# Sampled sequences: both heads' products of the incoming state in one step; shorter gaps between recurrence steps, with a bank booked apart from the gap

## The chip, the cores and the metric

The kernel runs on one core of a Trainium2 chip. A core has a matrix engine (TensorE; PE in the profile), three engines for elementwise work (VectorE or DVE, ScalarE or ACT, GpSimd or POOL) and DMA queues (SyncE or SP issues most of them). The metric is the device time of one execution in microseconds (us). The kernel before took 1620.5 us, the median of three runs that lie between 1619.76 and 1621.67.

## The reference, cut to what matters

One layer of a decoder trunk is computed for a prompt of 1024 tokens and for eight sampled sequences of 8 tokens, which share all weights. The part that the change touches is the RWKV-7 recurrence: eight heads of 64 channels, each with a 64x64 state.

```python
P = h @ lp["w_in"]
pr, pp, pg = jnp.split(P, [RWKV_COLS, RWKV_COLS + POOL_WIDTH], axis=-1)
o_r, s_shift, s_wkv, v_first = rwkv7_branch(pr, shift0[l], wkv0[l], v_first, lp)
o_p, s_pool = pool_branch(pp, pool0[l], pos0, lp)

def step(S, inp):                       # inside rwkv7_branch, once per token
    r_t, w_t, k_t, v_t, kk_t, a_t = inp
    sa = jnp.einsum("bhvk,bhk->bhv", S, -kk_t)
    S = (S * w_t[:, :, None, :]
         + sa[..., None] * (kk_t * a_t)[:, :, None, :]
         + v_t[..., None] * k_t[:, :, None, :])
    y = jnp.einsum("bhvk,bhk->bhv", S, r_t)
    return S, y
```

The prompt starts from a zero state. Each sampled sequence starts from a given state (`state_wkv`), so its 8 tokens need the products of r and of kk with that incoming state.

## The kernel before

**Two phases.** The tokens (1024 + 64 = 1088 columns) lie along the free dimension, features on the 128 partitions. Phase 1 multiplies by `w_in`, 34 blocks of 128 output columns, and runs the recurrence and the pooling branch among these products. Phase 2 (branch products, output projection, feed-forward, final norm) starts with products that read the recurrence's result. Every dense product is made of float32r matmuls in three terms (`mm3`: high x high, high x low, low x high), on three chunks of 362 to 364 columns. They write the PSUM tiles `mm`.

**The recurrence.** Two heads at a time share the 128 partitions (`HB` = partitions 0-63 and 64-127), so there are four head pairs, f = 0 to 3. The prompt goes in chunks of 64 tokens. Per head pair the steps are:
- `front` and `burst`: decays, keys and so on, elementwise and some products.
- `scores`: `unit(0)`, `bonus`, `unit(2)`, `unit(1)`. Units 0 and 1 are eight prompt chunks each, unit 2 is the sampled tokens. A unit makes its score products in groups of four chunks (two groups for a prompt unit, one for unit 2), each group into two PSUM banks, one a head; then it scales the keys in place (`bh`), transposes values and keys, and makes one more product.
- `inverse` (VectorE) and `level` (small 32x32 products): a triangular inverse.
- `affine`: `first(0)`, `second(0)`, `first(1)`, `second(1)`, each with two banks; they turn a chunk into one affine map of the state.
- `chain`: sixteen dependent steps through these maps. It keeps the two `wc` banks for itself meanwhile (`pace.held`).
- `sample`: the sampled tokens, from the incoming state `s0` (64 rows a head, 512 columns: 8 sequences x 64). `post`: group norm and gating.

**The order on TensorE is written out by the program.** TensorE's instructions keep the order in which the Python code issues them; the other engines are ordered by the framework. `Pace` is a planner that decides that order as the program is built. It keeps a clock `t` of estimated TensorE time, moved on by each matmul. `Pace.run` has one background generator (the dense products; each `yield` is one group of three matmuls) and four foreground generators, in this order: `chains`, `pools`, `heads`, `or_rows`. A foreground generator yields either a number of nanoseconds, and is due that much later, or a condition. Whenever a foreground generator is due it makes its next step; otherwise one more dense group is issued. So the number after a step is the distance, filled with dense products, to the next one.

**Two generators in one.** `both(a, fill)` merges two foreground generators into one, with `a` first. In `heads`, `lead` (burst and scores of f) goes with `sample(f-1)`, and `main` (inverse, level, affine of f) with `fill` (post of f-1, then front of f+1). For f = 0 `lead` runs alone, without `both`.

**Banks.** The recurrence, pooling and sampling steps share four PSUM banks, two called `w` and two called `wc`. `ps("w")` takes the one that the planner thinks is free first (`take`). After a step, `give` books each taken bank as free again at t + r, where r is the number that the step yields (at least 1500, at most 3600); for a step inside `both` it is `pace.gap`, which `both` sets to that same number. `free` says whether any bank is free by that estimate, and a step of `heads` inside `both` waits for it. Nothing of this is a hardware wait; the true waits are semaphores, and a step that is issued before its bank or data is ready makes TensorE wait.

The numbers that the change touches stand in `unit` (`yield 3500` after each score group), `affine` (`yield 3600` after `second`) and `sample`. Matmuls are all recorded at L204 (`mm`), transposes at L211 (`tr`); the copies and sums that empty the banks have lines of their own: L855 to L863 for the score groups, L1093 and L1100 for `sample`, L684 for the pooling steps, L1163 and L1184 for `post`.

Of the kernel before, what the change touches and what calls it, by code (L numbers as in the profile page):

```python
# [83 lines left out]
class Pace:  # L84
# [3 lines left out]
    def __init__(self):  # L88
        self.t = 0.0
        self.work = []  # L90
        self.dense = False
        self.taken, self.banks, self.gap, self.held = None, {"w": [0.0, 0.0], "wc": [0.0, 0.0]}, 1500, False

    def take(self):

# [6 lines left out]

    def free(self):
        return min(self.banks[x][0] for x in (["w"] if self.held else ["w", "wc"])) <= self.t

    def give(self, r):
        for tag in self.taken:
# [24 lines left out]
    def run(self, back, fore=(), until=lambda: False):  # L132
        self.back = back
        live = {i: 0.0 for i in range(len(fore))}
        busy = True
        while (live or busy) and not until():
            for i in sorted(live):
                r = live[i]
                if self.taken is not None and i and not self.free() and (i == 2 and not isinstance(r, Off) and not hasattr(r, "own") or i == 1 and not callable(r) and self.t < r + 1200):
                    continue  # L140
                if r() if callable(r) else r <= self.t:
                    if self.taken is not None:
                        self.taken, self.gap = [], 1500
                    try:
                        r = next(fore[i])
                        if self.taken:
                            self.give(min(max(self.gap if callable(r) else r, 1500), 3600))
                        live[i] = r if callable(r) else type(r)(self.t + r)
                    except StopIteration:
                        del live[i]  # L150
                    break
            else:
                r = "idle"
                if busy:
                    try:
                        r = next(back)
                    except StopIteration:
                        busy = False
                self.dense = r != "idle"
                if r == "idle" and live:  # L160
                    self.t += 100
# [9 lines left out]
class K:  # L171
# [647 lines left out]
    def unit(self, f, d, u):  # L819
# [22 lines left out]
        for a in range(0, C, 4):  # L842
# [3 lines left out]
            pss = [self.ps("w") for _ in HB]  # L846
# [4 lines left out]
            for h, (hs, ps) in enumerate(zip(HB, pss)):  # L851
                os = HB[1 - h]
# [4 lines left out]
                for b in range(2):  # L857
# [5 lines left out]
                            nc.scalar.activation(ao[rq, cu, :], pa[rq, :, 32:64], AF.Copy)  # L863
                    else:
                        nc.vector.tensor_tensor(ad[rq, 16, :], src[:, 0, :], strict[rq, 32 * b:32 * b + 32], op=ALU.mult)
            yield 3500
        bh = bk[:, cs, :, :].rearrange("p c s j -> p c (s j)")
        if prompt:
            nc.vector.tensor_tensor(bh, bh, end[:, cs].unsqueeze(2).to_broadcast([P, C, 128]), op=ALU.mult)
# [4 lines left out]
        ps, pa = self.ps("w"), self.ps("w") if prompt else None  # L874
        for i in range(C):
            for h, hs in enumerate(HB):
                c, os = c0 + i, HB[1 - h]
                self.mm(ps[hs, i * 64:(i + 1) * 64], v[hs, c * 64:(c + 1) * 64], ident[hs, hs], start=True, stop=True)
        if prompt:
            for i in range(C):  # L880
                for h, hs in enumerate(HB):
                    os = HB[1 - h]
# [6 lines left out]
        for a in range(0, C, 4):  # L889
            m = min(4, C - a)  # L890
            ps = self.ps("w")
# [4 lines left out]
        if prompt:  # L896
            yield 800
            ps = self.ps("w")
            for i in range(C):
                for h, hs in enumerate(HB):  # L900
                    os = HB[1 - h]
# [90 lines left out]
    def affine(self, f, d):  # L992
# [35 lines left out]
        for u in range(2):  # L1028
            first(u)
            yield 2500  # L1030
            second(u)
            self.done.add(("s", f, u))
            yield 3600

    def chain(self, f, d):

# [39 lines left out]
    def sample(self, f, d):  # L1076
# [14 lines left out]
            os = HB[1 - h]  # L1091
            self.mm(px[os, 0:64], ak[hs, 0, :], uv[hs, 0, h, :], start=True, stop=True, tile_position=(hs.start, os.start))
        nc.scalar.activation(x2, px[:, 0:64], AF.Copy)  # L1093
        for h, hs in enumerate(HB):
            os = HB[1 - h]
            if h:
                yield 2500
            ps, um = self.ps("w"), iv()
            self.mm(ps, ra[hs, 0, :, :].rearrange("p s j -> p (s j)"), s0[hs, :], start=True, stop=True)
            nc.vector.tensor_tensor(qv(um), qv(ps), qm.unsqueeze(2).to_broadcast([P, 8, 64]), op=ALU.mult)  # L1100
            nc.vector.tensor_reduce(xr[:, h, :], um.rearrange("p (q v) -> p v q", v=64), axis=AX.X, op=ALU.add)
            nc.vector.tensor_tensor(x[os], xr[os, h, :], x2[os], op=ALU.add)
        yield 9500 if f < 3 else 8000
        px = self.ps("w")
        for os in HB:
            self.mm(px[os, 0:64], z[os, 16, :], x[os, :], start=True, stop=True)
# [145 lines left out]
    def both(self, a, fill):  # L1252

        pace = self.pace
        live = [[a, pace.t], [fill, pace.t]]
        now = lambda: [x for x in live if (x[1]() if callable(x[1]) else x[1] <= pace.t) and (isinstance(x[1], Off) or pace.free())]
        some = lambda: bool(now())
        some.own = True
        while live:
            ready = now()  # L1260
            if not ready:
                yield some
                continue
            x = ready[0]
            try:
                r = next(x[0])
                x[1] = r if callable(r) else type(r)(pace.t + r)
                if pace.taken:
                    pace.gap = 1500 if callable(r) else r
                    yield some  # L1270
            except StopIteration:
                live.remove(x)
# [51 lines left out]
    def iv(self):  # L1324
        return self.p1.tile([P, 32, 32], F32, tag="iv", bufs=2, name=self.nm("iv"))
# [730 lines left out]
NC = 17  # L2056
FH = [(0, 512), (512, 576)]
FP = [(0, 512), (512, 288), (800, 288)]
LS = (2000, 2000, 2000, 1500)
FW = 5500  # L2060
WB = (2, 2)
# [77 lines left out]
```

## Time and profile before

| | |
|---|---|
| median of three runs | 1620.5 us |
| the profiled execution | 1620.03 us, its span 1618.2 us |
| mean granted TensorE clock | 0.996 of full speed |
| ScalarE, GpSimd busy | 736.1 us, 356.5 us |
| 64x512 products of `sample` (w<-hv,ra) | 16 instructions, 641 ns each in the middle |
| 64x64 products of `chain` (wc<-S,ra and wc<-ra,S) | 240 + 240 instructions, 218 ns each |

A profile row of the timeline gives start, duration, engine, line, operation, output tile <- input tiles, shape, and in brackets the idle time before it and what ended it. Tile names are the program's: `hx` and `whi`/`wlo` are dense products, `ra`, `ab`, `ak`, `uv`, `at`, `bk`, `z` belong to the recurrence, `px` and `plw` to pooling, `wt` is a row buffer and `hv` a scratch tile (in `sample` it is `s0` and the masked products). A matmul of float32 is two instructions, and one of less than 128x128 uses a part of the array. Rows of a table by windows give the window, the length, busy time (and count) of the engines asked for, the granted clock, the DMA share and GB/s; with all engines the order is PE, PEld, DVE, ACT, POOL.

### The profile page before, as it was taken

What the parts mean: (1) busy time and instruction counts of PE and PEld (TensorE: products, weight loads), DVE (VectorE), ACT (ScalarE), POOL (GpSimd) and SP (SyncE); (2) the same over time, 40 slices, a digit from 0 to 9 for tenths busy, and PEclk for the clock granted to TensorE, in tenths of its full rate; (3) what the DMA queues carried; (4) which work ended last, traced back from release to release, by engine and by line L of the source; (5) the groups of instructions that cost most, each with busy time, mean ns of one, the idle gap of its engine ahead of it and who ended that gap; (6) DMA issues with size and microseconds to landing.
All of it is one profiled execution on the core that took longest, in us unless ns stands there. A gap on an engine that the chain in (4) does not pass through costs nothing.

```text
span 1618.2 us, 35474 instructions
## 1 busy us (share of the span) xinstructions
PE 1583.4 (98%) x14331; PEld 1481.7 (92%) x14331; DVE 1022.9 (63%) x1747; ACT 736.1 (45%) x1491; POOL 356.5 (22%) x464
## 2 busy tenths in 40 slices
PE   5999999999999999999999999999999999999997
PEld 3999888998898889979989999999999999999997
DVE  5685674846565636244635597777555777787866
ACT  5543343344335433432325475554455765553323
POOL 3301200120001000101513322333233243521231
PEclk9999999999999999999999999999999999999998
DMA  9334423423423242746875466667666865674313
GB/s 336 110 119 145 140 65 107 132 83 115 126 101 115 76 138 89 294 144 216 332 261 175 144 199 215 206 223 256 234 209 234 312 201 186 197 265 154 100 40 111
DMA packets 123333, 279.43 MB, mean 173 GB/s; under 512 B 16769, under 2 KB 31105, under 8 KB 123169
## 3 DMA queue, kind: packets, MB, share of 16 engines
q1 hardware_dynamic: 107808, 228.52, 41.7%
q0 software_dynamic: 9312, 32.41, 6.0%
q10 hardware_dynamic: 6048, 16.23, 2.8%
q8 instruction: 113, 1.85, 0.5%
q14 instruction: 52, 0.42, 0.1%
HBM read 198.15 MB, written 78.95 MB: 171 GB/s over the span
## 4 chain that ended last, share of the span: by engine, by line
PE 61%; DVE 2%; issue 2%; ACT 2%; DMA 1%; POOL 1%; DVEq 0%; SPq 0%; ACTq 0%; POOLq 0%
PE pr L204 30%; PE mm L204 22%; PE w L204 4%; PE wc L204 4%; DVE hx L1815 0%; DMA wr<-in_w_ff 0%; POOL wlo L228 0%; PE wc L211 0%; DVE hx L1984 0%; DMA wraw<-in_w_ff 0%; PE w L211 0%; POOL wr L1788 0%; DMA d_th<-px 0%; ACT hx L1738 0%; ACT mr L1738 0%
## 5 line engine op out<-in xcount | busy, mean ns | idle before, releaser
L204 PE MATMUL mm<-hx,whi 128*128 128x362 f32 (+1 forms) x1920 | 504.8, 344 | 0.8 <-ACT px L573 0.8
L204 PEld LDWEIGHTS mm<-hx,whi 128*128 128x128 f32 x1920 | 330.1, 189 | 34.0 <-issue 16.1
L204 PE MATMUL pr<-mr,whi 128*128 128x272 f32 x1792 | 336.4, 287 | 0.5 <-DVE hx L1815 0.2
L204 PE MATMUL mm<-hx,wlo 128*128 128x362 f32 (+1 forms) x960 | 314.1, 327 | 0.0
L204 PEld LDWEIGHTS pr<-mr,whi 128*128 128x128 f32 x1792 | 280.8, 188 | 2.7 <-issue 2.7
L204 PE MATMUL pr<-mr,wlo 128*128 128x272 f32 x896 | 257.9, 288 | 0.0
L227 ACT ACTIVATE whi<-wraw 128x512 fp32r<-128x512 f32 x186 | 116.8, 629 | 222.1 <-PE mm L204 86.3
L228 DVE TENSOR_TENSOR wlo<-wraw,whi 128x512 fp32r<-128x512 f32 x145 | 107.5, 742 | 132.2 <-ACT whi L227 130.3
L204 PEld LDWEIGHTS mm<-hx,wlo 128*128 128x128 f32 x960 | 181.3, 189 | 0.0
L204 PE MATMUL pr<-hx,whi 128*128 128x272 f32 x896 | 168.8, 287 | 1.4 <-DVE rs L2010 0.8
L204 PEld LDWEIGHTS pr<-mr,wlo 128*128 128x128 f32 x896 | 168.6, 188 | 0.2 <-DVE wlo L228 0.2
L204 PE MATMUL mm<-mr,whi 128*128 128x272 f32 (+4 forms) x736 | 152.3, 301 | 0.0
L204 PEld LDWEIGHTS pr<-hx,whi 128*128 128x128 f32 x896 | 140.3, 188 | 2.7 <-ACT whi L227 1.0
L227 ACT ACTIVATE whi<-wr 128x512 fp32r<-128x512 f32 x138 | 86.3, 627 | 113.8 <-PE pr L204 76.3
L204 PE MATMUL pr<-hx,wlo 128*128 128x272 f32 x448 | 128.9, 288 | 0.0
L204 PEld LDWEIGHTS mm<-mr,whi 128*128 128x128 f32 x736 | 119.2, 188 | 3.0 <-issue 2.5
L204 PE MATMUL mm<-mr,wlo 128*128 128x272 f32 (+4 forms) x368 | 110.1, 299 | 0.0
L228 POOL TENSOR_TENSOR wlo<-wraw,whi 128x512 fp32r<-128x512 f32 x41 | 54.8, 1337 | 217.8 <-ACT whi L227 217.6
L228 DVE TENSOR_TENSOR wlo<-wr,whi 128x512 fp32r<-128x512 f32 x103 | 76.7, 747 | 18.3 <-ACT whi L227 18.2
L204 PE MATMUL pr<-t,whi 128*128 128x272 f32 x448 | 84.6, 287 | 0.0
L204 PEld LDWEIGHTS pr<-hx,wlo 128*128 128x128 f32 x448 | 84.3, 188 | 0.0
L204 PEld LDWEIGHTS pr<-t,whi 128*128 128x128 f32 x448 | 70.2, 188 | 0.8 <-issue 0.8
(466 smaller groups left out, 2711.0 us busy)
## 6 DMA issues: line engine op xcount, KB each, us to landing
wr<-in_w_ff SPq DMA_DIRECT2D x137, 256.0 KB, 3.5
hid<-d_ch POOLq DMA_DIRECT2D x72, 272.0 KB, 3.9
wraw<-in_w_ff SPq DMA_DIRECT2D x71, 256.0 KB, 3.2
wraw<-in_w_in SPq DMA_DIRECT2D x68, 256.0 KB, 3.1
d_ch<-hx SPq DMA_DIRECT2D x52, 272.0 KB, 3.8
hid<-in_w_ada_mlp SPq DMA_DIRECT2D x24, 512.0 KB, 6.5
d_th<-px SPq DMA_DIRECT2D x22, 544.0 KB, 3.1
wt<-d_x SPq DMA_DIRECT2D x20, 544.0 KB, 4.2
```

Of the source, the lines that this page charges most:

```text
L204: return self.nc.tensor.matmul(out, lhsT, rhs, **kw)
L227: nc.scalar.activation(hi, raw, AF.Copy)
L228: (nc.gpsimd if pool else nc.vector).tensor_tensor(lo, raw, hi.bitcast(F32), op=ALU.subtract)
```

## The change

`sample` issued the product of the two 64x64 operands and head 0's product of the incoming state in one step, and head 1's 2500 ns later. Now the 64x64 product goes alone, and 800 ns later both heads' products of the state go next to each other, into two banks; VectorE's work on each follows. The next step comes 11000 (9500 for f = 3) after that instead of 9500 (8000) after head 1's.

In `unit` the gap after a score group goes from 3500 to 2000, and in `affine` the gap after `second` from 3600 to 500. A new field `pace.est` lets a step inside `both` book its banks for another time than its gap: 3500, 3600 and 3600 at these three places. A step that is due then still waits in the planner for a bank that is free by estimate.

There are also a method `soon`, which may put off a step of the later generators where another one is due within `PAIR` ns, and the due time `some.due` that it reads; `PAIR` is 0.

```diff
@@ Pace.__init__
+        self.est = None
@@ Pace
+    def soon(self, live, i):
+
+        if not self.dense or i == 1:
+            return False
+        ts = [getattr(r, "due", lambda: None)() if callable(r) else None if isinstance(r, Off) else r for j, r in live.items() if j != i and j < 3]
+        return any(t is not None and self.t < t <= self.t + PAIR for t in ts)
@@ Pace.run
                 if r() if callable(r) else r <= self.t:
+                    if self.taken is not None and not isinstance(r, Off) and self.soon(live, i):
+                        continue
@@ unit
-            yield 3500
+            self.pace.est = 3500
+            yield 2000
@@ affine
             second(u)
             self.done.add(("s", f, u))
-            yield 3600
+            self.pace.est = 3600
+            yield 500
@@ sample
         nc.scalar.activation(x2, px[:, 0:64], AF.Copy)
-        for h, hs in enumerate(HB):
-            os = HB[1 - h]
-            if h:
-                yield 2500
-            ps, um = self.ps("w"), iv()
+        yield 800
+        pss = [self.ps("w") for _ in HB]
+        for hs, ps in zip(HB, pss):
             self.mm(ps, ra[hs, 0, :, :].rearrange("p s j -> p (s j)"), s0[hs, :], start=True, stop=True)
+        for h, ps in enumerate(pss):
+            os, um = HB[1 - h], iv()
             nc.vector.tensor_tensor(qv(um), qv(ps), qm.unsqueeze(2).to_broadcast([P, 8, 64]), op=ALU.mult)
             nc.vector.tensor_reduce(xr[:, h, :], um.rearrange("p (q v) -> p v q", v=64), axis=AX.X, op=ALU.add)
             nc.vector.tensor_tensor(x[os], xr[os, h, :], x2[os], op=ALU.add)
-        yield 9500 if f < 3 else 8000
+        self.pace.est = 3600
+        yield 11000 if f < 3 else 9500
@@ both
+        some.due = lambda: min([x[1] for x in live if not callable(x[1]) and not isinstance(x[1], Off)], default=None)
...
                 if pace.taken:
-                    pace.gap = 1500 if callable(r) else r
+                    pace.gap = pace.est or (1500 if callable(r) else r)
+                    pace.est = None
                     yield some
@@ constants
+PAIR = 0
```

## The prediction

> **What bounds it.** I read the engine table first, then TensorE's waits between 60 and 760 us (the stage in which the recurrence runs among the projections), then that stage's timeline.
>
> ```profile
> span 1618.2 us, 35474 instructions
> PE 1583.4 (98%) x14331; PEld 1481.7 (92%) x14331; DVE 1022.9 (63%) x1747; ACT 736.1 (45%) x1491; POOL 356.5 (22%) x464
> ...
> PE wc L211 <- DVE px L684: 1.4, 1, 1.4
> PE wc L204 <- DVE wt L1184: 1.1, 1, 1.1
> PE w L204 <- ACT hv L979: 0.9, 1, 0.9
> ...
> PE wc L204 <- ACT wt L333: 0.5, 1, 0.5
> PE wc L204 <- ACT wt L725: 0.4, 1, 0.4
> PE w L204 <- ACT wt L1163: 0.4, 1, 0.4
> PE wc L204 <- DVE px L684: 0.3, 1, 0.3
> ```
>
> TensorE works 98% of the span. From the first score group to the recurrence's end it waits seven times, 5.0 us in all. So the end is set by the sum of what TensorE does, not by the length of the recurrence: a step that goes sooner lets a projection product go later, and the sum stays. The end of the stage says the same:
>
> ```profile
> 737.82 0.27 PE L211 MATMUL w<-kct,sw 128*128 128x128 f32 x1
> ...
> 741.74 1.38 DVE L1202 TENSOR_TENSOR hx<-wt,hx 128x576 fp32r<-128x576 f32 x1
> ...
> 753.42 0.49 PE L204 MATMUL w<-hx,whi 128*128 128x362 f32 x2
> ```
>
> The recurrence's last TensorE work is at 737.8, its result is in SBUF at 743.1, and the first product that reads it starts at 753.4. There are 10 us of slack already, all filled with projection products. More slack buys nothing.
>
> **Part 1: both heads' products of the incoming state in one step (sample).** Each product multiplies 64 rows of the state, 512 columns wide. Before, they go 3.8 us apart. In the same shape the front step issues its w2 and a2 products side by side, on rows 0-63 and 64-127, into two banks:
>
> ```profile
> 548.62 0.33 PE L204 MATMUL w<-uv,ak 64*64 64x64 f32 x4
> 548.88 1.12 PE L204 MATMUL w<-hv,ra 64*128 64x512 f32 x2
> 549.93 0.59 PE L204 MATMUL mm<-hx,whi 128*128 128x362 f32 x2
> ...
> 552.70 1.12 PE L204 MATMUL w<-hv,ra 64*128 64x512 f32 x2
> 553.75 0.33 PE L204 MATMUL wc<-S,ra 64*64 64x64 f32 x4
> ...
> 534.56 0.69 PE L204 MATMUL w<-wt,sw 64*128 64x512 f32 x1
> 534.57 0.69 PE L204 MATMUL wc<-wt,sw 64*128 64x512 f32 x1
> 535.10 0.59 PE L204 MATMUL w<-wt,sw 64*128 64x512 f32 x1
> 535.10 0.59 PE L204 MATMUL wc<-wt,sw 64*128 64x512 f32 x1
> 535.62 0.60 PE L204 MATMUL mm<-hx,whi 128*128 128x362 f32 x2
> ...
> L204 PE MATMUL w<-hv,ra x16: 589/641/693, 231.0 to 700.1; 64*128 64x512 f32 x16
> ```
>
> One state product alone takes 548.88 to 549.93, 1.05 us, and the other 552.70 to 553.75, again 1.05. The front's pair takes 534.56 to 535.62, 1.06 us for both: the two halves of the array worked at once. The new step issues its two products adjacent, on the same two row halves, into two banks, so 2.10 becomes 1.06. The x16 are two instructions for each of eight products, so four head pairs gain: 4 x 1.04 = 4.2 us off TensorE's path. The number of visits to small tiles stays at two (the old first visit held the 64x64 product and head 0; now that product goes alone). The ends are 0 (the products run one after another) and 4.2; I take 4.2 because the front's rows have the same shape, rows and form.
>
> By the Trainium skill ("TensorE: Matmul & The Clock Gate", section "Step-by-step: what each phase is for") TensorE pulls weight loads ahead but keeps matmuls in program order. By that rule the second instruction of head 0 would hold back the first of head 1; the rows at 534.56 and 534.57, of two different products, do not look like it. What it would make of the sum is the in-order rival below.
>
> The second of the two banks may be the one that the 64x64 product has just filled, since the chain of states keeps the two "wc" banks at that time:
>
> ```profile
> 549.71 0.24 ACT L1093 ACTIVATE x<-w 128x64 f32<-128x64 f32 x1
> ```
>
> It is emptied at 549.95, 1.3 us after that product began. The new step starts at least two 0.5 us groups of projection products after it (800 ns of the planner), at about 1.4 us: no wait to 0.2 us, and I take nothing. The old wait for ACT L1163 (0.4) belongs to the same place in the last head and may go; I leave it among the re-drawn ones. VectorE's work on the products is the same six steps, and the next consumer is 11 us of the planner's time off.
>
> **Part 2: score groups 2000 apart instead of 3500, affine 500 instead of 3600.** Nothing is added to any engine; five gaps per head pair shrink by 1.5 us and two by 3.1 us. Their steps wait for a bank estimate of 3500 or 3600 only where no bank is free. Is the data there when they go?
>
> ```profile
> 295.80 0.37 PE L204 MATMUL w<-ra,bk 64*128 64x128 f32 x1
> ...
> 300.56 0.37 PE L204 MATMUL w<-ra,bk 64*128 64x128 f32 x1
> ...
> 300.21 0.27 ACT L861 ACTIVATE iv<-wc 32x128 f32<-32x128 f32 x1
> ...
> 305.45 0.97 PE L204 MATMUL wc<-kct,wt 64*64 64x64 f32 x26
> ```
>
> Here the groups start 4.8 us apart; after it, about 3.3. The second group takes the other two banks. The transposes at 305.45 come about 3 us sooner, at 302.5, and reuse the first group's banks, empty at 300.5: 2 us of margin. In head pairs 1 to 3 the step is hidden this way; their first unit has only two banks (the chain holds the rest) and stays nearly as it is. Head pair 0 is tighter, VectorE being crowded there:
>
> ```profile
> 80.00:120.00 40.00, 39.95 (x307) 36.38 (x307) 34.80 (x55) 18.48 (x47) 3.36 (x12) 1.00 0.36 119
> ...
> 117.42 1.23 DVE L869 TENSOR_TENSOR bk<-bk,end 128x1024 f32<-128x1024 f32 x1
> ...
> 120.24 0.60 PE L211 MATMUL w<-kct,bk 128*128 128x128 f32 x4
> ...
> 179.50 1.94 DVE L935 STREAM_TRANSPOSE iv<-iv 128x512 f32<-128x512 f32 x2
> 183.37 0.82 PE L204 MATMUL w<-hv,hv 32*32 32x32 f32 x74
> ```
>
> The scaled keys are ready at 118.65 and TensorE transposes them at 120.24, 1.6 us later. Two gaps ahead of that transpose shrink by 3.0 us; if VectorE (87% busy in this slice) does not move its work up, TensorE waits 1.4 us. The inverse ends at 181.4 and its first product starts at 183.4: 2.0 us of margin, of which one gap (1.5) lies between the last scores and it, so at most a fraction of a microsecond there. Both together are 0 to 1.9 us; I take 0.7, a little under the middle, as VectorE takes ready work first in most rows. In the affine steps the first product of the second half needs nothing of the step just before it; the cover of two banks emptied since the first half is 5 us old by then. Nothing.
>
> **Part 3: what does nothing.** PAIR is 0, so soon() asks for a due time that is later than now and not later than now: it never holds a step back, and due only feeds it. The est field only books banks. In head pair 0 the leading steps do not go through both(), so their banks are booked for 2000 and not 3500; that is within the 1.4 us above. No DMA is added or moved past another by hand; the loads of the next head pair go earlier on SP with its steps, and no wait of TensorE in this stage is for a DMA.
>
> **Part 4: the waits are drawn anew.** Every recurrence step after 106 us shifts against the pool steps, so the seven waits above (5.0 us) will stand elsewhere. The worst is a pile-up at 504 to 512, where a pool step, a spread and a level step fall due together with no projection between them:
>
> ```profile
> 504.00:508.00 4.00, 3.05 (x69) 1.00 0.00 0
> 508.00:512.00 4.00, 2.62 (x29) 0.83 0.43 135
> 512.00:516.00 4.00, 4.00 (x61) 0.74 0.07 21
> 680.00:684.00 4.00, 4.00 (x116) 1.00 1.02 416
> ```
>
> It idles 0.95 + 1.38 = 2.3 us, and the granted clock then falls to 0.83 and 0.74 for 4 us each, 0.7 + 1.0 us more: 4.0 in all. With the clock, 6.7 us are drawn anew. None of them may come back, or twice as much; I take the same again, 0, since as many steps meet as before.
>
> **The sum.** -4.2 + 0.7 + 0 = -3.5 us. The profiled execution took 1620.03 us (1618.2 of span and 1.8 around it), 0.5 under the median 1620.5 and within its three runs: 1616.5 us.
>
> **Rivals.** *In-order products* (the two products of the new step overlap only in their middle instruction): three half products of 0.53, 1.58 instead of 2.10, gain 2.1; 1620.0 - 2.1 + 0.7 = 1618.6. The front's four rows speak against it, and that the matmuls' ends are modelled speaks a little for it.
> *The pile-up goes*: its 4.0 us do not come back elsewhere, 1612.5. For it: one coincidence in the whole stage made it. Against: shorter gaps make coincidences likelier.
> *New waits eat it*: head pair 0 pays its 1.9 and another 2 us arise where steps crowd, such as both halves of the affine going back to back: 1620.0 - 4.2 + 3.9 = 1619.7.
> *Slower: more pile-ups.* With steps 0.5 to 2 us apart, a pool or post step that falls due between them leaves TensorE without a projection product, at 4.0 us a time. One new one brings the sum to 1620.5, two to 1624.5: it takes two, with the old one still there. Against it speaks the window 680 to 684, where chain and affine already run 4 us without a projection product, with TensorE busy and the clock at 1.00. The Trainium skill ("TensorE: Matmul & The Clock Gate", section "What's actually happening") ties the low clock to an idle window of about 3.4 us; the rows agree in so far as it fell only after the one place with 2.3 us idle.
> *The change does nothing but reorder* is the zero end of part 1: the products serial, 1620.7 with the 0.7.
>
> **Chances.** Forecast (1616.5, own range 1614.5 to 1618.5) 0.47; in order 0.08; pile-up gone 0.15; eaten 0.13; slower 0.13; reorder only 0.04. What a measurement of this kernel can tell from no change is 0.2%, 3.2 us: faster means below 1617.3. That holds for three quarters of the forecast's range (0.36) and the pile-up case (0.15): 0.52 with a hair of the in-order case. Slower is 0.13, the rest, 0.35, is the same. The range 1612.0 to 1621.5 takes in all but the slower case and the low half of the pile-up case.
>
> **What will show it.** Part 1: four pairs of w<-hv,ra whose two products start within 0.05 us of each other and end 1.06 later; else the in-order rival shows 1.6. Part 2: score groups about 3.3 us apart in units 1 and 2; a wait behind DVE bk near 117 us or behind DVE hv near 180 if head pair 0 pays. Part 4: a windows table by 4 us with another list of idle slices and clocks below 0.9. The last recurrence step earlier than 737.8, with the first product of the next stage some 4 us earlier, no more. The forecast is wrong if idle of TensorE between 100 and 760 us differs by more than 3 us, or if the pairs run in turn.

## The result, and the profile after

The changed kernel is slower: 1650.99 us, the median of four runs (1649.55 to 1651.72), against 1621.09 (1619.76 to 1623.48). The ratio is 1.0183 (95% interval 1.017 to 1.0195), about 30 us. The forecast was 1616.5. The profiled execution took 1651.52 us.

First the engine table and TensorE's row of forty slices, from the profile's page after the change:

```profile
span 1649.7 us, 35486 instructions
PE 1590.3 (96%) x14331; PEld 1488.5 (90%) x14331; DVE 1020.7 (62%) x1747; ACT 737.0 (45%) x1491; POOL 354.0 (21%) x464
...
PE   6999999997999699989999999999999999999997
```

TensorE's busy time grew by 7 us, its share fell by two points, and slices 9 and 13 (near 390 and 550 us) have holes. TensorE's waits between 60 and 800 us (total, times, longest) name them:

```profile
PE w L214 <- issue: 22.2, 2, 13.8
PE mm L214 <- ACT px L616: 2.2, 1, 2.2
PE mm L214 <- DVE px L1420: 2.1, 1, 2.1
PE w L214 <- ACT z L1000: 1.5, 1, 1.5
```

Two waits hold 22.2 of some 31 us; before, no wait was above 1.4. TensorE's timeline shows which instructions waited, and the ends of the phase:

```profile
379.15 1.13 PE L214 MATMUL w<-hv,ra 64*128 64x512 f32 x4
393.54 1.55 PE L214 MATMUL w<-px,plw 128*128 128x364 f32 x2 [8.43 <-issue]
556.67 1.55 PE L214 MATMUL w<-px,plw 128*128 128x364 f32 x2 [13.80 <-issue]
742.94 0.42 PE L221 MATMUL w<-kct,sw 128*128 128x128 f32 x1
785.13 0.49 PE L214 MATMUL w<-hx,whi 128*128 128x362 f32 x2
```

Both are the first product of a pool step (`pools`: `w<-px,plw`), of channel groups 1 and 3. The first product of phase 2 starts at 785.1 instead of 753.4, so the loss lies in phase 1; the recurrence, whose steps were to go on sooner, ends 5 us later.

The profile calls the cause "issue". VectorE's timeline shows the cause itself. A pooling column ends with sums over `px` (L653 to L666 after the change, L643 to L656 before; L664 or L654 is the last write of the pool step's operand). These are some of VectorE's rows after the change:

```profile
378.08 1.23 DVE L653 TENSOR_TENSOR d<-px 128x1038 f32<-128x1038 f32 x1
379.23 0.34 DVE L654 TENSOR_TENSOR psm<-psm 128x183 f32<-128x183 f32 x1
379.49 0.74 DVE L776 TENSOR_TENSOR bk<-wt,wt 64x576 f32<-64x576 f32 x1
...
382.37 1.24 DVE L653 TENSOR_TENSOR px<-d 128x1036 f32<-128x1036 f32 x1
...
383.78 1.28 DVE L1112 TENSOR_TENSOR hv<-w,kct 128x512 f32<-128x512 f32 x2
...
386.33 1.35 DVE L789 SCALAR_TENSOR_TENSOR wt<-wt,part,wt 128x1088 f32<-128x1088 f32 x1
...
392.03 1.21 DVE L663 SCALAR_TENSOR_TENSOR px<-px,px 128x1024 f32<-128x1024 f32 x1
393.27 0.17 DVE L664 COPY px<-zf 128x3 f32<-128x3 f32 x1
```

The sums of group 1 take from 378.08 to 393.44, 15.4 us, and TensorE's product starts 0.1 us later. Among them stand the burst of the next head pair (L761 to L789) and the sample's work (L1112 to L1114). Before, the same sums took 9.4 us, with work of `post` and `affine` among them, and did not touch the burst:

```profile
352.06 1.23 DVE L643 TENSOR_TENSOR d<-px 128x1038 f32<-128x1038 f32 x1
...
359.47 1.22 DVE L653 SCALAR_TENSOR_TENSOR px<-px,px 128x1024 f32<-128x1024 f32 x1
...
379.28 0.43 DVE L751 TENSOR_SCALAR wt<-wt 128x512 f32<-128x512 f32 x1 [2.53 <-ACT wt L725]
```

The recurrence did run ahead: burst 2 begins at 367 instead of 379 us. The pooling column, a projection product that went later for it, moved the other way: its sums begin at 378 instead of 352. So they met. The pool step is issued a fixed time of the planner after the sums (9800 ns in group 1), whatever VectorE does meanwhile; TensorE came to it 7.0 us after the sums' start and waited 8.4. Both halves of that wait changed: before, TensorE came 14.0 us after the start of sums that took 9.4. In group 3 it is the sums alone: they take from 533.26 to 556.57, 23.3 us (10.1 before), and TensorE came 9.6 us after their start (10.7 before). The banks are not what it waited for: VectorE's last reads of the banks of the sample's pair (L1112) end at 385.1 and 547.1 us, 8 and 10 us before the two waits do. The windows around both, the first with all engines (PE, PEld, DVE, ACT, POOL), the others with TensorE alone:

```profile
384.00:390.00 6.00, 1.11 (x12) 0.74 (x11) 5.95 (x14) 1.31 (x4) 0.93 (x1) 1.00 0.40 120
...
552.00:556.00 4.00, 0.00 (x0) 0.50 0.44 139
556.00:560.00 4.00, 3.33 (x10) 0.50 0.00 0
```

TensorE idles while VectorE is 99% busy (5.95 of 6.00 us), and goes on at half clock (0.50).

An account of phase 1 (40 to 784 us, from windows of 4 us): idle time, and the clock's loss, which is busy time x (1 - granted clock). Before: 5.9 and 1.5 us. After: 30.8 and 10.0. Idle +24.9, clock +8.5, the products' 4.2 us off: +29.2 of the 31.7 us by which the first product of phase 2 is late. What makes the other 2.5 us is not settled. And 3.4 of the 8.5 us of clock are not the change's: the half clock from 79.4 to 86.2 us stands ahead of the first place where the two kernels' TensorE instructions differ (109.4 us before). The changed execution was 3.2 us late there already.

### The profile page after: what moved, and what is told of

Its sections match the earlier page's. It is cut to its first block, busy times and chain, and to the rows that moved or that the text cites. A ratio compares the mean times of both kernels' runs of the same rounds, so it can differ in the third digit from the quotient of the medians.

```text
span 1649.7 us, 35486 instructions
## 1 busy us (share of the span) xinstructions
PE 1590.3 (96%) x14331; PEld 1488.5 (90%) x14331; DVE 1020.7 (62%) x1747; ACT 737.0 (45%) x1491; POOL 354.0 (21%) x464
## 4 chain that ended last, share of the span: by engine, by line
PE 64%; issue 3%; DVE 2%; DMA 1%; ACT 1%; POOL 1%; DVEq 0%; ACTq 0%; POOLq 0%; SPq 0%
PE pr L214 32%; PE mm L214 23%; PE w L214 5%; PE wc L214 4%; DMA wraw<-in_w_out 1%; DMA hx<-d_opl 1%; DVE hx L1830 0%; POOL wlo L238 0%; ACT whi L237 0%; PE wc L221 0%; PE w L221 0%; DVE hx L1999 0%; POOL wr L1803 0%; POOL hx L2027 0%; ACT mr L1753 0%
## 5 line engine op out<-in xcount | busy, mean ns | idle before, releaser
L214 PE MATMUL mm<-hx,whi 128*128 128x362 f32 (+1 forms) x1920 | 512.4, 349 | 4.9 <-ACT px L616 2.2
L214 PEld LDWEIGHTS mm<-hx,whi 128*128 128x128 f32 x1920 | 333.9, 191 | 38.3 <-issue 15.8
L237 ACT ACTIVATE whi<-wr 128x512 fp32r<-128x512 f32 x138 | 86.2, 627 | 113.3 <-PE pr L214 81.7
```

Of the source, the lines that this page charges most:

```text
L214: return self.nc.tensor.matmul(out, lhsT, rhs, **kw)
L237: nc.scalar.activation(hi, raw, AF.Copy)
```

## The experiments

The theory after the first look, M: the shorter gaps let the recurrence run ahead, its VectorE work meets the pooling sums, and TensorE waits at the pool steps. Its rivals: the new sample step makes the meeting (S); or any running ahead loses, wherever the columns stand (C). Each run's idle time and clock loss in phase 1 are counted as above, on its profiled execution. Each ratio is to the kernel before as it ran beside that run (medians of 1621.1 to 1623.2 us).

| run | median us | ratio (95% interval) | idle, clock loss | waits at pool steps 1, 3 |
|---|---|---|---|---|
| before | 1621.1 | | 5.9, 1.5 | none over 1 |
| changed | 1651.0 | 1.0183 (1.017 to 1.0195) | 30.8, 10.0 | 8.4, 13.8 |
| e1 new sample only | 1623.1 | 1.0015 (1.0000 to 1.0031) | 10.6, 1.6 | none over 2 |
| e2 gaps only | 1653.4 | 1.0191 (1.0174 to 1.0208) | 29.5, 10.6 | 7.6, 10.3 |
| e3 changed, columns earlier | 1636.7 | 1.0092 (1.0069 to 1.0114) | 14.6, 12.0 | none, 4.6 |
| e4 before, columns later | 1625.6 | 1.0017 (1.0007 to 1.0028) | 7.2, 4.7 | 0.9, none |
| e5 score gap only | 1639.9 | 1.0111 (1.009 to 1.0132) | 12.5, 9.2 | 2.5, 2.4 |
| e6 affine gap only | 1621.3 | 1.0007 (0.999 to 1.0023) | 6.3, 5.0 | none |
| e7 before, column 1 on the burst | 1626.2 | 1.0026 (1.0013 to 1.004) | 7.8, 3.2 | 1.6, none |
| e8 changed, columns apart | 1647.5 | 1.015 (1.0112 to 1.0189) | 21.2, 15.6 | none, 2.0 |
| e9 changed, old score gap | 1625.2 | 1.0012 (0.9999 to 1.0024) | 10.0, 6.5 | none, 3.0 |
| e10 before, pool step 3 later | 1622.9 | 0.9996 (0.9984 to 1.0007) | 5.9, 0.0 | none |
| e11 new sample, pool step 3 later | 1622.7 | 1.0003 (0.9987 to 1.002) | 7.3, 5.1 | none |
| e12 columns apart, rows' loads held | 1640.2 | 1.0105 (1.0074 to 1.0136) | 18.1, 2.9 | none, 2.0 |
| e13 changed, burst held | 1631.6 | 1.0055 (1.0039 to 1.007) | 9.4, 8.2 | 3.7, none |
| e14 columns apart, half the pooled rows | 1638.1 | 1.008 (1.0054 to 1.0106) | 13.0, 13.2 | none, 2.0 |

**e1: the sample step alone.** The kernel before with the new `sample` (without its `pace.est`).

```diff
-        for h, hs in enumerate(HB):
...
+        yield 800
+        pss = [self.ps("w") for _ in HB]
...
-        yield 9500 if f < 3 else 8000
+        yield 11000 if f < 3 else 9500
```

> The kernel before with the new sample alone: both heads' products of the state in one step, the gaps after score groups and in affine as before. Theory M (meeting: the shorter gaps move burst and sample of the next head pair onto the pooling columns' sums on VectorE, and TensorE waits in the pool step for those sums): the meeting does not come about, no wait of TensorE above 2.5 us between 100 and 760 us, four pairs of products in about 1.06 us each, 1617 us (1621.1 less 4.2). Rival S (the new sample itself makes the meeting, because its two wide multiplies and two sums now come together on VectorE and hold two banks): a pool step waits 5 us or more, 1635 us or more.

The pairs run side by side and no pool step waits long, so S falls. But the 4.2 us do not show in the time: idle time and clock loss grew by 4.8. In TensorE's waits (60 to 800 us) nothing stands out; they are small ones, drawn anew:

```profile
PE w L204 <- DVE px L654: 1.9, 1, 1.9
PE w L204 <- ACT uv L1007: 1.8, 1, 1.8
PE mm L204 <- ACT px L606: 1.2, 1, 1.2
```

**e2: the gaps alone.** The changed kernel with the old `sample`.

```diff
-        yield 800
-        pss = [self.ps("w") for _ in HB]
...
+            if h:
+                yield 2500
```

> The changed kernel with the sample of before: only the gaps after score groups (2000) and after affine's second (500), with the banks booked for 3500 and 3600. Theory M: both waits of the changed kernel in pool steps of channel groups 1 and 3 are there, 8 and 14 us give or take 3, and the products of the state run singly: 1651 + 4.2 = 1655 us. Rival S: no such wait, 1621 us give or take 4.

The whole loss and both waits are there without the new sample step (the second, 10.3 us, a little under its range). The gaps make it.

**e3: the changed kernel with its pooling columns earlier.** The columns of groups 1 and 3 each stand one gate earlier, by a new list.

```diff
-        for g in range(4):
-            jobs += [Q[g], G[2 * g], G[2 * g + 1]] if g < 3 else [G[6], Q[3], G[7]]
+        jobs += [Q[0], G[0], Q[1], G[1], G[2], G[3], Q[2], G[4], G[5], Q[3], G[6], G[7]]
```

> The changed kernel with the pooling columns of groups 1 and 3 one gate block (12 us of products) earlier in the dense order, nothing else. Theory M: their sums on VectorE end before burst of head pairs 2 and 3 begins, the waits of 8.4 and 13.8 us and the low clock behind them (about 6 us) go: 1651 - 22 - 6 = 1623 us, 1617 to 1627 as other waits are drawn. Rival B (the waits come from the banks or from the shorter gaps by themselves, wherever the pool steps stand): waits of 5 us or more remain, 1640 us or more.

The two waits went and 14 us came back: 1636.7 lies between the two forecasts. One meeting is left: group 3's sums now meet the work of `post` and of the affine step (14.1 us from 493.76), in TensorE's timeline and window:

```profile
507.98 1.55 PE L214 MATMUL wc<-px,plw 128*128 128x364 f32 x2 [4.58 <-issue]
...
504.00:508.00 4.00, 0.02 (x1) 0.75 0.81 277
```

The rest is clock (12.0 us against 1.5, of which 3.3 near 80 us, ahead of anything that the change moves) and small waits at the end of the phase.

**e4: the kernel before with its columns later**, group 1's by two gates and group 2's by one (the expectation says two for both).

```diff
-        for g in range(4):
-            jobs += [Q[g], G[2 * g], G[2 * g + 1]] if g < 3 else [G[6], Q[3], G[7]]
+        jobs += [Q[0], G[0], G[1], G[2], G[3], Q[1], G[4], Q[2], G[5], G[6], Q[3], G[7]]
```

> The kernel before, none of the change in it, with the pooling columns of groups 1 and 2 two gate blocks later in the dense order, so that group 1's sums fall on burst and sample of head pair 2 (VectorE rows from 379 us on). Theory M: the pool step of group 1 waits 5 to 10 us for its sums and the clock falls behind it, 1628 to 1636 us. Rival B (it takes the shorter gaps or the new bank times): no wait above 2.5 us in that pool step, 1618 to 1625 us.

No such wait: this placement missed the burst. Group 1's sums ran from 402.06 to 406.92 with nothing among them. The run says that a late column as such costs little, and nothing on the meeting. From here on the columns were placed by VectorE's order of instructions.

**e5 and e6: the two gaps, one at a time.** The kernel before with `pace.est` and one of the two splits.

```diff
+            self.pace.est = 3500
-            yield 3500
+            yield 2000
```

> The kernel before, with the score step's 3500 ns split into 2000 ns and a 3500 ns stay of its banks, and with nothing else of the change (the two products in turn, the affine step's 3600 ns whole). Theory M (a pooling group's sums meet other VectorE work, and the pool step, which is issued a fixed time later, waits for them): with the score part alone 7.3 us of other VectorE work stands in VectorE's order among the sums of group 1 and 7.7 us among those of group 3 (an estimate from the elements of each instruction at the rate of the 128x1038 row, 1.23 us); in the changed kernel it is 9.6 and 14.6 us with waits of 8.4 and 13.8 us, in the kernel with pooling columns earlier it is 7.1 us at group 3 with a wait of 4.6 us. So waits of 3 to 6 us at both pool steps, and 1632 to 1642 us. Rival C (any running ahead of the recurrence loses the same, wherever the columns stand): about 1650 us, as with all gaps.

```diff
             self.done.add(("s", f, u))
-            yield 3600
+            self.pace.est = 3600
+            yield 500
```

> The kernel before, with the affine step's 3600 ns split into 500 ns and a 3600 ns stay of its banks, and nothing else of the change. Theory M: 4.5 and 0.8 us of other VectorE work stand among the sums of groups 1 and 3 (5.1 and 0.7 us before), so no wait above 2 us at a pool step, and 1619 to 1627 us, with the other waits drawn anew. Rival C: clearly slower, 1635 us or more, since the recurrence steps go on 3.1 us sooner at each affine step.

The affine split, the larger cut (3.1 us, twice per head pair), does nothing to the time. The score split alone costs 18 us, with waits of 2.5 and 2.4 us at the pool steps (a little under the expected 3 to 6) and 9.2 us of clock. The time of e5 lies in M's range and 10 us under C's. But e6 is no test of C: in it the recurrence does not run ahead. Its burst 2 begins later than before (379.28):

```profile
386.70 0.43 DVE L761 TENSOR_SCALAR wt<-wt 128x512 f32<-128x512 f32 x1 [2.55 <-ACT wt L735]
```

In e5 it begins at 363.5. So it is the score gap that lets the recurrence run ahead, and whether running ahead costs by itself stays open here. The two waits of e5 and the 8.4 and 13.8 of both splits together are not a sum: what counts is what stands among the sums.

**e7: the meeting, made in the kernel before.** Nothing of the change; group 1's column one gate later, onto burst 2.

```diff
-        for g in range(4):
-            jobs += [Q[g], G[2 * g], G[2 * g + 1]] if g < 3 else [G[6], Q[3], G[7]]
+        jobs += [Q[0], G[0], G[1], G[2], Q[1], G[3], Q[2], G[4], G[5], G[6], Q[3], G[7]]
```

> The kernel before, without any part of the change; only the pooling column of group 1 stands one gate later in the order of the projection columns, so that its sums stand among the work of burst 2 in VectorE's order: 9.3 us of other work among the sums of group 1, where it was 5.1. Theory M: a wait of 6 to 9 us at group 1's pool step with a clock loss of 2 to 4 us behind it, and 1628 to 1636 us, though no recurrence step was let go sooner. Rival C (it is the running ahead and not the meeting): 1619 to 1624 us and no such wait.

The direction is right, the size is not. The sums met the burst and took 13.7 us (379.35 to 393.09), as expected, but TensorE came to the step only 12.3 us after their start, where in the changed kernel it came after 7.0:

```profile
393.19 0.85 PE L204 MATMUL w<-px,plw 128*128 128x364 f32 x2 [1.59 <-issue]
```

So a wait is the sums' time less the time until TensorE comes, and M had left the second out. About 2 us of the difference is VectorE's queue ahead of the sums: in the changed kernel ScalarE's last copy of the column ended at 375.8 and the sums began at 378.1, behind the burst; here it was 0.3 us. What makes the other 3 us was not found.

**e8: all gaps, columns away from everything**: groups 1, 2 and 3 earlier by one, one and two gates.

```diff
-        for g in range(4):
-            jobs += [Q[g], G[2 * g], G[2 * g + 1]] if g < 3 else [G[6], Q[3], G[7]]
+        jobs += [Q[0], G[0], Q[1], G[1], G[2], Q[2], G[3], G[4], Q[3], G[5], G[6], G[7]]
```

> The changed kernel with all its gaps, with the pooling columns of groups 1, 2 and 3 ahead of where they stood by one, one and two gates: Q0 G0 Q1 G1 G2 Q2 G3 G4 Q3 G5 G6 G7. By VectorE's order 1.3, 1.6, 3.2 and 1.3 us of other work stand among the four groups' sums (before 1.5, 5.1, 1.2, 0.7; changed 1.3, 9.6, 4.3, 14.6). Theory M: no wait above 2.5 us at any pool step, and 1618 to 1628 us; the whole loss at the two pool steps and most of the clock loss is gone. Rival C: 1640 us or more, with the idle time spread over other steps. Were it faster than the kernel before, the sums being apart would be the version to keep.

M holds at the place and fails in the time, which is what C foretold (1640 or more, with idle time at other steps). The waits at the pool steps are 2.0 us and less, yet only 3.5 us came back. Two other losses took the place: clock (15.6 us, of which 6.8 behind 2.0 us of idle time near 482), and three waits of 12.9 us together, two of them (9.8 us) at 716 to 737:

```profile
645.75 0.60 PE L214 MATMUL mm<-hx,whi 128*128 128x362 f32 x2 [3.09 <-ACT px L616]
...
720.93 0.97 PE L214 MATMUL mm<-hx,whi 128*128 128x362 f32 x2 [5.09 <-ACT px L616]
...
736.88 0.97 PE L214 MATMUL mm<-hx,whi 128*128 128x362 f32 x2 [4.68 <-DVE px L1419]
...
719.89 0.63 ACT L237 ACTIVATE whi<-wraw 128x512 fp32r<-128x512 f32 x1 [5.53 <-DMA hx<-d_opl]
```

The expectations of e12 and e14 take the first two waits for one of 8.2 us at the end of the phase. At 645.75 ScalarE's eviction stood behind other work of ScalarE's, and no load was waited for. At 719.89 ScalarE waits 5.5 us for a weight that lands among the pooled rows' loads (`hx<-d_oph`, `hx<-d_opl`), and with it the gate's eviction and TensorE. This is a second theory, N: 14 loads of 544 KB (7.6 MB) stand at the end of the columns. With the recurrence ahead, the columns end later, and there is no recurrence work left to spread them. The share of TensorE's `mm` products in the 8 us of heaviest loads fits it, first in the kernel before, then in the changed one (busy us of 8, clock, DMA share, GB/s):

```profile
664.00:672.00 8.00, 3.99 (x23) 1.00 1.03 409
...
720.00:728.00 8.00, 7.78 (x43) 1.00 1.02 411
```

The DMA engines are full in both (shares of 1.03 and 1.02). Before, TensorE spent half of the time on recurrence products and issued about half as many `mm` products (23 against 43), which need the weights.

**e9: the change without its score part.**

```diff
-            self.pace.est = 3500
-            yield 2000
+            yield 3500
```

> The changed kernel with the score step's 3500 ns whole again; the two products side by side, the affine step's split and the rest as changed. Theory M (only the meeting of a group's sums with other VectorE work, which the score part brings about, and the end of the phase that comes late with it, make the loss): 4.5 and 1.4 us of other work among the sums of groups 1 and 3 (by VectorE's order), so no wait above 2 us at a pool step, none above 1 us on the rows' loads at the end of the phase, and 1617 to 1625 us: the 4.2 us of the products less what the other waits, drawn anew, take. Rival C (any running ahead costs): 1635 us or more.

From 1651.0 to 1625.2, with no wait at the rows' loads. One pool step waits 3.0 us (2 were named as the limit), and the products' 4.2 us are again taken by waits and clock. They were not won whole either: in the first pair head 1's product began 1.8 us after head 0's (237.32 and 235.52), so these two ran one after the other. The loss hangs on that one number in `unit`. But burst 2 begins at 387.7 here, so e9, like e6, has no running ahead in it and does not part M from C.

**e10 and e11: pool step 3 later**, in the kernel before and with the new sample step alone.

```diff
-            yield (8500, 9800, 9800, 10800)[g]
+            yield (8500, 9800, 9800, 14000)[g]
```

> The kernel before, with group 3's pool step 14000 ns after its sums are issued instead of 10800. Before, the sums took 10.1 us and TensorE came to the step as they ended, amid 2.3 us of idle time and 3.4 us at half clock (504 to 514 us). If that pile-up is the wait for the sums, it goes: 1616 to 1619 us. If it is drawn elsewhere again: 1620 to 1624 us.

> The kernel before with the two products side by side, and group 3's pool step 14000 ns after its sums are issued. The products alone gave 4.2 us of TensorE time and lost 4.8 us to waits and clock, 3.4 us of them at 504 to 512 us, where the step met its sums (11.6 us). If that wait goes and nothing takes its place: 1617 to 1620 us, faster than both kernels. If the waits are drawn anew as before: 1621 to 1625 us.

In both, the idle time around that step is less: 0.8 us instead of 2.3 in e10, none instead of 1.9 in e11. It was not the step's wait for its sums, though: in the kernels without the delay TensorE came 10.7 and 14.9 us after the start of sums that took 10.1 and 11.6. In e11 a wait of 2.1 us stands at 526.8 instead, and in e10 the idle time of the whole phase is 5.9 us as before. The profiled execution of e10 had no low clock at all between 40 and 784 us and took 1618.4 us, the lowest of its ten runs (1618.4 to 1625.5). The medians did not move: neither can be told from the kernel before. The gain of the pile-up's end is smaller than the spread of the runs.

**e12: the recurrence rows' loads held back** (e8 with one line more).

```diff
         yield lambda: "op" in self.done
+        yield 20000
         for j in range(3):
```

> The changed kernel with the pooling columns apart, and the six loads of the finished recurrence rows (3.3 MB, 711 to 718 us there) held back by 20000 ns more, nothing else. Theory N (with the recurrence ahead, the rows' loads of the output columns, 7.6 MB in all, fall to a stretch in which TensorE does columns alone, and the weights of the columns wait behind them): the two waits of 8.2 us (the gate's eviction behind a weight that landed late) and 4.7 us fall to 6 us or less together, and 1636 to 1643 us. If the rows' loads are not the cause: 1645 to 1650 us and the same waits.

The edit did not do what it says: in both kernels the loads begin 2.8 to 2.9 us after the last of the pooled rows' (708.35 and 711.18 us in e8, 703.92 and 706.80 here). Probably the planner's 20000 ns had passed by then. At the end of the phase the waits were 2.1 and 4.7 us (a third, of 3.1, stands at 642.8). TensorE's instructions come in the same order in e8 and e12, and so do SyncE's, yet the median fell by 7 us, with runs from 1634.8 to 1645.1 and a clock loss of 2.9 us instead of 15.6 in the profiled one. This decides nothing on N; it says that some 7 us in the time of such a kernel can come without any change of TensorE's order.

**e13: the meeting taken away, the columns left where the change put them.** The burst's steps and the sample's pair wait in the planner until a pool step whose sums are issued has gone.

```diff
             yield (8500, 9800, 9800, 10800)[g]
+            self.done.add(("pz", g))
...
+    def calm(self):
+        return all(("pool", g) not in self.done or ("pz", g) in self.done for g in range(4))
...
             yield step(1800)
+            yield self.calm
...
                 yield step(1700)
+                yield self.calm
...
             yield step(1400)
+            yield self.calm
...
         yield 800
+        yield self.calm
         pss = [self.ps("w") for _ in HB]
```

> The changed kernel with all its gaps and with the columns in the changed order; only the burst's steps and the sample's pair of products are held until the pool step of a group whose sums have been issued has gone. By VectorE's order 6.2 us of other work are left among the sums of group 1 and 3.0 among those of group 3, where it was 9.6 and 14.6 (an estimate from the elements). Theory M: the waits at the two pool steps fall from 8.4 and 13.8 us to under 5 and under 4 us, and the time to 1626 to 1640 us. Rival C (the columns' or the recurrence's places make the loss, not what VectorE does among the sums): the waits stay, 1645 us or more.

As expected: 1631.6 us, 19 us back, with all gaps of the change. Group 1's sums stand where they stood in the changed kernel, and less stands among them; group 3's begin at 522 us instead of 533, take 10.4 us, and TensorE comes 13.9 us after their start. VectorE's first and last sums of group 1, TensorE's two pool steps, and its largest wait:

```profile
377.83 1.23 DVE L653 TENSOR_TENSOR d<-px 128x1038 f32<-128x1038 f32 x1
...
388.32 0.17 DVE L664 COPY px<-zf 128x3 f32<-128x3 f32 x1
...
388.55 0.88 PE L214 MATMUL w<-px,plw 128*128 128x364 f32 x2 [3.75 <-DVE px L664]
...
535.90 0.78 PE L214 MATMUL w<-px,plw 128*128 128x364 f32 x2
```

The sums took 10.7 us, TensorE came 7.0 us after their start, as in the changed kernel, and waited the difference, 3.7. This time the profile names VectorE. Group 3's wait of 13.8 us is gone; so are the waits at the end of the phase. Where VectorE was to blame, taking its other work away gave most of the time back, and C's 1645 us or more did not come. The hold also takes back a part of the running ahead: burst 2 begins at 367.2 us as in the changed kernel, but burst 3 at 534.8 instead of 529.2. So e13 shows the cause of the two waits, and not that running ahead costs nothing by itself. The first product of phase 2 is still 12.7 us later than before: 3.5 us of idle time and 6.7 of clock (half of it at 79 to 86 us, ahead of the change), less the products' 4.2, and some 7 us that this account does not hold.

**e14: half of the pooled rows' loads.** e8 without the four loads of the low halves; the output columns' products read the high half in its place.

```diff
-            for i in range(2):
-                t = self.row(self.hx, "hx", 16, F32R)
-                nc.sync.dma_start(t.bitcast(F32), self.d_op[i][j])
-                self.op[i].append(t)
+            t = self.row(self.hx, "hx", 16, F32R)
+            nc.sync.dma_start(t.bitcast(F32), self.d_op[0][j])
+            for i in range(2):
+                self.op[i].append(t)
```

> The changed kernel with the pooling columns apart, and without the four loads of the low halves of the pooled rows (2.2 of 7.6 MB): the output columns read the high half in place of the low one, so the output is not the reference's, and TensorE does as many products. Theory N: the waits of 8.2 and 4.7 us at 716 to 736 us fall to 6 us or less together and the half clock behind them goes, 1634 to 1643 us. If the loads are not the cause: both waits stay, 1640 to 1650 us.

Of the two waits of e8 at the end of the phase, 9.8 us together, one of 1.5 us is left, and no low clock follows it. The third, at 645.75 in e8, stays as it was:

```profile
648.85 0.60 PE L214 MATMUL mm<-hx,whi 128*128 128x362 f32 x2 [3.09 <-ACT px L616]
...
729.13 0.60 PE L214 MATMUL mm<-hx,whi 128*128 128x362 f32 x2 [1.53 <-DVE px L1419]
```

So N is borne out for these waits, with one profiled execution of each kernel (e12, with all loads, had 6.7 us there). The time, 1638.1, is in the expected range, but says little: e12 took 1640.2 with all the loads, and low clock elsewhere (17.1 us long behind 482 us) hides part of the gain.

**What the runs leave of C.** In all runs in which the recurrence ran ahead (burst 2 at 363 to 369 us) time was lost, also where the sums met less or nothing: 15 us in e3, 26, 18 and 15 in e8, e12 and e14, and 8 in e13. What was lost there is clock and waits at other places. So the meeting makes the two waits, the largest part of the changed kernel's loss; that a recurrence that runs ahead would cost nothing without it is not shown.

## Why the prediction was wrong

**Part 1 was right in the mechanism and in its size.** Four pairs, each of 1.06 us to the next product (379.15 is one; the others are at 225.80, 540.68 and 691.66). The in-order rival fell: in the changed kernel the first instructions of both heads start at 379.15 and 379.16, the second ones at 379.68 and 379.69. The prediction had it from the Trainium skill's sentence on program order ("TensorE: Matmul & The Clock Gate", section "Step-by-step: what each phase is for"). The measurement goes against that reading of it; in which order the program asks for the four is not on record, so the sentence itself is not shown wrong. But "4.2 us off TensorE's path" is not 4.2 us off the time; e1 gave none of it.

**Part 2 was right on the margins it looked at.** Score groups start 3.3 us apart (286.51, 289.79, transposes at 293.08), and neither wait feared in head pair 0 appeared, so its 0.7 us was not spent. It was wrong in "Nothing is added to any engine" as a reason to stop: nothing was added, but VectorE's work was moved. The part asked only whether each moved step finds its own data and banks. It did not ask whose data stand behind the moved step's work on VectorE.

**Part 4 is the step that failed**: "I take the same again, 0, since as many steps meet as before". The waits and the clock, 6.7 us by its count, grew by 33 (30.8 + 10.0 against 5.9 + 1.5 in phase 1). The reason behind it, in the first part, was "a step that goes sooner lets a projection product go later, and the sum stays". It holds for TensorE alone. Some of the products that go later are pooling columns with 3 to 8 us of VectorE sums behind them and a step due at a fixed time; the steps that go sooner are followed by a burst. e2, e5 and e9 show that the score gap brings this about, e13 that the meeting makes the two waits of 22.2 us. The rest of the 33 us is mostly clock, 3.4 us of it ahead of the change, and why a recurrence that runs ahead loses time where nothing meets (e8) is shown for the end of the phase only.

**Part 3** named what does nothing; no run speaks against it. Its sentence that no wait in this stage is for a DMA was true of the kernel before and no longer of the changed one: at 729 us ScalarE waits 2.6 us for a load, and TensorE 2.2 us behind it. By e8 and e14 the same shift moved the rows' loads to where TensorE does columns alone.

**The rivals.** The slower one had the right sign and part of the mechanism, steps that crowd. Its price, 4.0 us a pile-up, came from the one that the trace showed, and its reason, that TensorE has no projection product between the steps, is not what happened: products were there, but stood in TensorE's order behind a step that waited for VectorE. The places cost 8.4 and 13.8 us. "The pile-up goes" could be tried by itself (e10): the idle time there shrinks and the median stays.

"More slack buys nothing" was right, and it was the hint: a change that can only move work, in a stage whose time is a sum, has little to gain and can lose wherever the moved work meets a fixed time.

No version tried beats the kernel before.

## What to carry to other kernels

When steps are let go sooner in an order written out by hand, follow their work on every engine, and ask which fixed due time stands behind the engine that gets crowded; that TensorE's own work is unchanged says nothing about it. Place a step that is due a fixed time after another engine's work by that engine's order of instructions: count what stands among them, and take the time until TensorE comes off it. A wait that the profile puts down to "issue" is to be held against the last write of the operand on the other engines.

## What the runs showed of the hardware

Stretches of half clock come in steps of 3.41 us. In windows of 0.5 us their lengths, over all profiles between 40 and 790 us, are 3.4, 6.8, 10.2, 13.7 and 17.1 us. One of the shortest is in the kernel before, the longest in e14; their first and last windows, the kernel before first:

```profile
510.50:511.00 0.50, 0.50 (x3) 0.66 0.85 299
...
514.00:514.50 0.50, 0.50 (x6) 0.93 0.00 0
```

```profile
482.50:483.00 0.50, 0.05 (x1) 0.96 0.00 0
...
500.00:500.50 0.50, 0.50 (x5) 0.98 0.98 400
```

Each step costs a busy TensorE 1.7 us (half of 3.41). A long wait is not needed. In e3 the clock fell for 10.2 us behind one wait of 0.71 us:

```profile
644.87 0.60 PE L214 MATMUL mm<-hx,whi 128*128 128x362 f32 x2 [0.71 <-ACT px L616]
...
644.00:648.00 4.00, 3.29 (x18) 0.74 0.39 136
648.00:652.00 4.00, 4.00 (x73) 0.50 0.23 73
652.00:656.00 4.00, 4.00 (x15) 0.50 0.00 0
```

In the changed kernel it fell for 6.8 us behind a wait of 0.65 us at 78 us:

```profile
78.04 0.60 PE L214 MATMUL mm<-hx,whi 128*128 128x362 f32 x2 [0.65 <-ACT px L583]
...
80.00:84.00 4.00, 4.00 (x15) 0.50 0.73 212
```

The kernel before waited longer at the same step and kept its clock:

```profile
77.82 0.59 PE L204 MATMUL mm<-hx,whi 128*128 128x362 f32 x2 [0.82 <-ACT px L573]
...
80.00:84.00 4.00, 3.95 (x25) 1.00 0.78 257
```

The Trainium skill ("TensorE: Matmul & The Clock Gate", section "What's actually happening") describes a free-running window of 3413 ns; the lengths agree with it. That the clock falls after an idle window of about 3.4 us, as the same section has it, does not cover these rows: fractions of a microsecond were enough, and not each time. What decides it was not found. It makes the price of a short wait anything from its own length to some 5 us more, and no sum over small waits can be better than that.
